# One step of a polynomial moved to GpSimd, K's placement to SyncE, and a new start, in a grouped-query attention kernel

**Chip, cores, metric.** One core of a Trainium2 chip (trn2). The metric is the device time of the whole program in microseconds (us): the median of several executions, each compared with executions of the kernel before on the same chip. A profiled execution also has a *span* in its trace.

## The reference

```python
q: (8, 8, 1024, 64)   k, v: (8, 2, 1024, 64)   float32; 4 query heads share one K and V
scores = (1/sqrt(64)) * q @ k^T
attn   = exp(scores - max) / sum(exp(scores - max))
output = attn @ v
```

There are 64 heads, each done as two *jobs* of 512 queries. A job has eight score tiles of 128 keys x 512 queries, so 1024 tiles ("cells") in all. Scores are small, so the kernel skips the maximum.

## The kernel before

TensorE makes each score cell into PSUM. Cells of kind A go to ScalarE, two per ACTIVATE. Cells of kind D go to VectorE: an eviction that scales the score into the bits of a bfloat16 power of two, then a correction of the mantissa for a whole group of cells:

```python
GROUP = 8
POOL_STEP = -1                       # no step of the chain on GpSimd
def exp_curve(g, m, step):           # all on VectorE
    if step == 0:   nc.vector.tensor_scalar(out=z, in0=pd, scalar1=0x7F, op0=ALU.bitwise_and)  # mask
    elif step == 1: nc.vector.tensor_scalar(out=y, in0=z, scalar1=CURVE_A / 128.0,
                                            scalar2=CURVE_B, op0=ALU.mult, op1=ALU.add)        # linear factor
    elif step == 2: nc.vector.tensor_tensor(out=y, in0=z, in1=y, op=ALU.mult)                  # product
    else:           nc.vector.tensor_tensor(out=pd, in0=pd, in1=y, op=ALU.add)                 # sum
```

A planner inside the kernel (`make_plan`) decides at build time which cells are A and which D, and in what order each engine works. It books a duration for every operation. Each engine then executes its list strictly in order.

Q and K are cast to bfloat16 through scratch memory by GpSimd's DMAs, transposed on load by SyncE's DMAs, and K is then copied to its two places:

```python
def place_k(b, g, side, parity):
    nc.gpsimd.dma_start(out=ksets[b % 2][...], in_=kT[(b, g)][...])      # 4 for each K, 60 in all
...
    for n in range(HALF // PIECE):
        at(th - 8.0 - 10.0 * spare + n, transpose_q, b, h, n)            # SyncE; th: planned first use
```

The first head does not wait for that path: TensorE transposes it, after 26 warm-up matmuls on a tile of zeros, and VectorE copies K to all its places.

The softmax here doesn't subtract the row's maximum and nothing guards it: scores larger than these inputs give would overflow.

Of the kernel before, what the change touches and what calls it, by code (L numbers as in the profile page):

```python
# [11 lines left out]

CURVE_A, CURVE_B = 0.32988085, -0.33401025

GROUP = 8
POOL_STEP = -1


def make_plan(nj, nkc):
# [5 lines left out]


    QK, PV, P1, NORM = 0.216, 0.1225, 0.603, 0.555
    EXP, AND, LINE, PRODUCT = (0.065, 0.4265), (0.20, 0.133), (0.20, 0.133), (0.16, 0.27)
    CHAIN = (AND, LINE, PRODUCT, PRODUCT)
    FROM_PE, FROM_ACT, FROM_DVE, FROM_POOL = 0.26, 0.17, 0.10, 0.15  # L30
    LIVE_A, LIVE_D, PENDING, PER_JOB, LEAD, RAMP, AHEAD, FIRST_PV = 28, 5, 16, 2, 6, 3, 0.08, 2.0
    INF = 1e9
    FIRST_LOAD, EACH_LOAD = 3.5, 4.0
    ops = []
    pe = act = dve = 0.0
    a_free, bank, obank_free = [0.0, 0.0], [0.0, 0.0], [0.0, 0.0]
# [18 lines left out]
    while normed < nj:  # L55
# [32 lines left out]
        for q, p, kind in ((normq, 0, "norm"), (p1q, 1, "p1"), (chainq, 2, "chain")):  # L88
            if q:
                at = q[0][0]  # L90
                if kind != "chain" or q[0][3] != POOL_STEP:
                    at = max(dve, at)
                best = min(best or (INF,), (at, p, kind, 0))
        if cur and job_d >= nj and not p1q:
# [2 lines left out]
        if kind == "qk":  # L97
            t = best[4]
            pe = t + QK
            j = job_d if arg else job_a  # L100
            cell = j * nkc + todo[j].pop(0)
            if not arg:
                if open_a is None:
                    slot = first_free(a_free)
                    a_id += 1
                    live["A"] += 1
                    open_a = {"slot": slot, "t": a_free[slot], "cells": []}
                    a_free[slot] = INF
                o = open_a
                ops.append((t, "qk", cell, "A", a_id, o["slot"], len(o["cells"])))  # L110
                o["cells"].append(cell)
                home[cell] = ("A", a_id)
                if len(o["cells"]) == 2 or not any(todo[job_a:]):
                    act = max(act, pe + FROM_PE)
                    ops.append((act, "exp", a_id, tuple(o["cells"])))
                    act += EXP[0] + EXP[1] * len(o["cells"])
                    a_free[o["slot"]] = act + FROM_ACT
                    uses[("A", a_id)] = len(o["cells"])
                    for x in o["cells"]:
                        ready[x] = act + FROM_ACT  # L120
                    open_a = None
            else:
                taken[j] += 1
                k = first_free(bank)
                bank[k] = INF
                pending += 1
                ops.append((t, "qk", cell, "D", k, 0, 0))
                p1q.append((pe + FROM_PE, cell, k))
        elif kind == "open":
            o = first_free(obank_free)  # L130
            obank[arg] = o
            obank_free[o] = INF
            open_jobs.append(arg)
            rem[arg] = list(range(nkc))
            next_job += 1
        elif kind == "pv":
            s, c = arg
            cell = s * nkc + c
            opens = len(rem[s]) == nkc
            rem[s].remove(c)  # L140
            done = not rem[s]
            ops.append((t, "pv", s, cell, opens, done, obank[s]))
            pe = t + PV
            h = home[cell]
            uses[h] -= 1
            if not uses[h]:
                live[h[0]] -= 1
            if done:
                open_jobs.remove(s)
                normq.append((pe + FROM_PE, s))  # L150
        elif kind == "norm":
            s = normq.pop(0)[1]
            ops.append((t, "norm", s))
            dve = t + NORM
            obank_free[obank[s]] = dve + FROM_DVE
            normed += 1
        elif kind == "p1":
            _, cell, k = p1q.pop(0)
            if not cur:
                d_id += 1  # L160
                live["D"] += 1
            ops.append((t, "p1", cell, k, d_id, len(cur)))
            dve = t + P1
            bank[k] = dve + FROM_DVE
            cur.append(cell)
            home[cell] = ("D", d_id)
            if len(cur) == GROUP:
                chainq.append((dve, d_id, cur, 0))
                cur = []
        elif kind == "flush":  # L170
            chainq.append((dve, d_id, cur, 0))
            cur = []
        else:
            _, g, cells, step = chainq.pop(0)
            ops.append((t, "chain", g, len(cells), step))
            end = t + CHAIN[step][0] + CHAIN[step][1] * len(cells)
            dve = end if step != POOL_STEP else dve
            if step + 1 < len(CHAIN):
                at = end + FROM_POOL if step == POOL_STEP else end
                at += FROM_DVE if step + 1 == POOL_STEP else 0.0  # L180
                chainq.insert(0, (at, g, cells, step + 1))
            else:
                pending -= len(cells)
                uses[("D", g)] = len(cells)
                for x in cells:
                    ready[x] = dve + FROM_DVE
# [4 lines left out]
def kernel(  # L191
# [7 lines left out]
    nc = tc.nc  # L199
# [17 lines left out]
    NQS = QBS // 128  # L217
    E1 = D + 1
    PIECE = 256
    WARM = 26  # L220
    SECOND = 0.45
    CAST_GAP = 3.0
    scale = 1.0 / math.sqrt(D)
    bits_scale = 128.0 * scale * math.log2(math.e)
    bits_bias = 128.0 * 127.0
# [4 lines left out]

    jobs = [(b, h, side) for b in range(B) for h in range(H) for side in range(2)]
    plan = make_plan(len(jobs), NKC)

    const_pool = ctx.enter_context(tc.tile_pool(name="constp", bufs=1))
    scr_pool = ctx.enter_context(
# [19 lines left out]
    apools, dbanks, obanks = psum_pools("aps", 2), psum_pools("dps", 2), psum_pools("ops", 2)  # L255

    blank = const_pool.tile([128, 128], BF16)
    nc.vector.memset(blank, 0.0)  # L258
    ident = const_pool.tile([128, 128], BF16)
    make_identity(nc, ident)  # L260
    vsets, ksets = [], []
# [11 lines left out]

    def at(t, f, *args):
        events.append((t, len(events), f, args))

    qT = {}
    kT = {}
# [24 lines left out]
        transpose(("k", b, g), kT[(b, g)], n)  # L303

    def place_k(b, g, side, parity):
        nc.gpsimd.dma_start(  # L306
            out=ksets[b % 2][
                side * D : (side + 1) * D, g, side, parity * HALF : (parity + 1) * HALF
            ],
# [18 lines left out]
    def first_loads():  # L328
# [46 lines left out]
        for n, half in enumerate(halves):  # L375
            nc.scalar.copy(out=hk[:, half, 0:2, :], in_=fk[:, half])  # L376
            nc.vector.tensor_copy(
                out=hq[:, half], in_=fq[:, half].rearrange("p c two d -> p c (two d)")
            )
            turn_k(0, half)  # L380
            keep_warm(2)
            for c in range(NHC)[half]:
                nc.tensor.transpose(tq[:, c * 128 : (c + 1) * 128], hq[:, c, :], ident)  # L383
            keep_warm(2)
            if n == 0:
                cast(("q", 0, 2), q[0, 2])
        for half in halves:
            cols = slice(half.start * 128, half.stop * 128)
            nc.scalar.copy(out=qT[(0, 0)][:, cols], in_=tq[:, cols])  # L389
            put_k(0, 0, half)  # L390
        def second():
            every = slice(0, NHC)
            turn_k(1, every)
            for side, parity in ((0, 1), (1, 0), (1, 1)):
                put_k(side, parity, every)

        nc.vector.tensor_copy(out=hk[:, :, 2, :], in_=fk[:, :, 0, :])
        at(SECOND, second)

    p_of = {}  # L400
    psum = {}
# [43 lines left out]

    def exp_curve(g, m, step):
        pd = groups[g][:, 0:m]
        if step == 0:
            z = tmp_pool.tile([128, GROUP, QBS], U16, name="z")[:, 0:m]
            temps[g] = [z]  # L450
            nc.vector.tensor_scalar(  # L451
                out=z, in0=pd, scalar1=0x7F, scalar2=None, op0=ALU.bitwise_and
            )
        elif step == 1:
            y = tmp_pool.tile([128, GROUP, QBS], FP16, name="y")[:, 0:m]
            temps[g].append(y)
            nc.vector.tensor_scalar(  # L457
                out=y,
                in0=temps[g][0],
                scalar1=CURVE_A / 128.0,  # L460
# [3 lines left out]
            )  # L464
        elif step == 2:
            z, y = temps[g]
            nc.vector.tensor_tensor(out=y, in0=z, in1=y, op=ALU.mult)  # L467
        else:
            y = temps.pop(g)[1]
            groups.pop(g)  # L470
            nc.vector.tensor_tensor(out=pd, in0=pd, in1=y, op=ALU.add)  # L471

    def output_mms(s, cell, opens, closes, bk):
        b, h, side = jobs[s]
# [13 lines left out]
    def normalise(s):  # L488
# [1 line left out]
        o = ops_of.pop(s)  # L490
        rec = recip_pool.tile([128, NQS], FP32, name="rec")
        nc.vector.reciprocal(out=rec, in_=o[:, :, D])  # L492
        if side == 0:
            stage[(b, h)] = ostage_pool.tile([128, NQS, 2, D], FP32, name="ost")
        nc.vector.tensor_tensor(  # L495
            out=stage[(b, h)][:, :, side, :],
# [9 lines left out]
            in_=stage[(b, h)][:, :, sides],  # L506
        )

    first_use = {}
    run = {"qk": score, "exp": exps, "p1": exp_bits, "chain": exp_curve,  # L510
           "pv": output_mms, "norm": normalise}
    for op in plan:
        if op[1] == "qk":
            first_use.setdefault(op[2] // (2 * NKC), op[0])
        elif op[1] == "norm":
            b, h, side = jobs[op[2]]
            if op[2] >= len(jobs) - 2:
                at(op[0] + 0.01, put_out, b, h, slice(side, side + 1))
            elif side:
                at(op[0] + 1.5, put_out, b, h, slice(0, 2))  # L520
        at(op[0], run[op[1]], *op[2:])

# [4 lines left out]
    for b in range(B):  # L527
        for h in range(H):
# [8 lines left out]
            if h % HPG == 0:  # L537
# [6 lines left out]
                    for parity in range(2):  # L544
                        at(th - 6.0 - 9.0 * spare, place_k, b, g, side, parity)
                for two in range(2):
                    at(th - 4.0 - 8.0 * spare + two, place_v, b, g, two)
    casts.sort(key=lambda e: e[0])
    latest = 1e9
    for n in reversed(range(len(casts))):  # L550
# [3 lines left out]
    for t, key, src in casts:  # L554
        t = max(t, soonest)
        soonest = t + 2.0
        at(t, cast, key, src)
    with tc.manual_schedule():
        first_loads()
        for _, _, f, args in sorted(events, key=lambda e: e[:2]):  # L560
# [31 lines left out]
```

## Time and profile before

Time before: 393.41 us (three runs, 393.38 to 393.47). The one run that left the first trace took 395.51 us, with a span of 393.7 us.

| | busy, of a span of 393.7 us | what it does |
|---|---|---|
| ScalarE (ACT) | 380.7 us, 97% | 411 exponentials, 822 cells |
| TensorE (PE) | 371.0 us, 94% | scores, outputs |
| VectorE (DVE) | 366.2 us, 93% | 202 cells, 128 normalisations |
| GpSimd (POOL) | 107.1 us, 27% | DMA issues |

A group line of the page reads: line, engine, operation, output<-input, shapes, count | busy time, mean ns of one | idle time of the engine just before, and what ended it. The prediction below shows these lines and reads them.

### The profile page before, as it was taken

The page shows a single profiled execution, that of the slowest core. Times are in us where ns is not written, and L with a number is a line of the kernel's source. Part 1 is how long each engine was busy: PE and PEld are TensorE (multiplying, and loading weights), DVE is VectorE, ACT ScalarE, POOL GpSimd, SP SyncE. Part 2 cuts the span into 40 slices and gives each one's busy share as a digit, 9 for nine tenths or more (in the row PEclk, how much of TensorE's full clock was granted, in tenths as well). Part 3 has the DMA queues.
Part 4 walks back from the last instruction along what each step waited for, and adds up shares of the span by engine and source line. Part 5 has one row for each costly group of instructions (what it writes and reads, how often), then busy time and mean ns, then how long its engine had stood idle before and what let it go on. Part 6 is the DMA issues. An engine that isn't in the chain of part 4 may idle for free.

```text
span 393.7 us, 12506 instructions
## 1 busy us (share of the span) xinstructions
PE 371.0 (94%) x5166; PEld 234.3 (60%) x5166; DVE 366.2 (93%) x573; ACT 380.7 (97%) x416; POOL 107.1 (27%) x184
## 2 busy tenths in 40 slices
PE   7989999999999999999999999999999999999995
PEld 5435556566666566566566566566556556556664
DVE  3799999999999999999999999999999999999992
ACT  4799999999999999999999999999999999999994
POOL 4285241413205032141413305032331416000000
PEclk9999999999999999999999999999999999999999
DMA  7499995756959559394665868468595658520113
GB/s 120 87 169 203 140 142 101 148 80 126 156 100 148 109 111 148 91 156 86 123 107 116 143 117 132 105 115 134 103 133 105 130 87 148 101 72 28 55 55 82
DMA packets 101992, 45.39 MB, mean 115 GB/s; under 512 B 66256, under 2 KB 99536, under 8 KB 100688
## 3 DMA queue, kind: packets, MB, share of 16 engines
q0 software_dynamic: 21600, 17.05, 34.9%
q1 hardware_dynamic: 79792, 27.29, 30.5%
q8 instruction: 40, 0.66, 0.7%
q10 hardware_dynamic: 544, 0.26, 0.2%
q14 instruction: 16, 0.13, 0.1%
HBM read 25.17 MB, written 27.00 MB: 133 GB/s over the span
## 4 chain that ended last, share of the span: by engine, by line
ACT 81%; PE 11%; issue 6%; DMA 1%; DVE 0%
ACT pa L427 80%; PE aps L416 5%; PE ops L479 4%; PE dps L416 2%; DMA fk<-in_k_dram 1%; DVE kset L350 0%; PE dps L341 0%; ACT qT L389 0%; PE ops L368 0%; PE dps L383 0%; DVE ost L495 0%; ACT hk L376 0%; DVE rec L492 0%
## 5 line engine op out<-in xcount | busy, mean ns | idle before, releaser
L427 ACT ACTIVATE pa<-aps 128x1024 bf16<-128x1024 f32 x411 | 378.0, 1064 | 3.9 <-PE aps L416 3.8
L416 PE MATMUL aps<-qT,kset 128*128 128x512 bf16 x822 | 245.8, 380 | 15.8 <-ACT pa L427 13.8
L479 PEld LDWEIGHTS <-pa 128*128 128x128 bf16 x3288 | 137.6, 98 | 61.1 <-issue 1.1
L479 PE MATMUL ops<-vset,pa 128*128 128x65 bf16 x3288 | 149.1, 194 | 0.0
L436 DVE TENSOR_SCALAR pd<-dps 128x512 uint16<-128x512 f32 x202 | 130.9, 682 | 3.7 <-PE dps L416 3.1
L416 PEld LDWEIGHTS <-kset 128*128 128x128 bf16 x1024 | 82.6, 98 | 73.4 <-issue 37.4
L286 POOL DMA_DIRECT2D scr_q<-in_q_dram x63 | 34.4, 545 | 201.5 <-PE aps L416 152.2
L416 PE MATMUL dps<-qT,kset 128*128 128x512 bf16 x202 | 71.4, 383 | 1.2 <-DVE kset L350 0.9
L495 DVE TENSOR_TENSOR ost<-ops,rec 128x256 f32<-128x256 f32 x128 | 54.3, 424 | 4.4
L471 DVE TENSOR_TENSOR pd<-pd,y 128x4096 uint16<-128x4096 uint16 (+1 forms) x26 | 57.8, 2224 | 0.3
L467 DVE TENSOR_TENSOR y<-z,y 128x4096 f16<-128x4096 uint16 (+1 forms) x26 | 57.7, 2220 | 0.1
L479 PEld LDWEIGHTS <-pd 128*128 128x128 bf16 x808 | 36.5, 97 | 18.3 <-DVE pd L471 0.6
L479 PE MATMUL ops<-vset,pd 128*128 128x65 bf16 x808 | 41.3, 193 | 0.0
L306 POOL DMA_DIRECT2D kset<-kT x60 | 34.5, 584 | 1.4 <-issue 0.4
L457 DVE TENSOR_SCALAR y<-z 128x4096 f16<-128x4096 uint16 (+1 forms) x26 | 31.5, 1210 | 0.0
L451 DVE TENSOR_SCALAR z<-pd 128x4096 uint16<-128x4096 uint16 (+1 forms) x26 | 31.3, 1202 | 0.0
L492 DVE RECIPROCAL rec<-ops 128x4 f32<-128x4 f32 x128 | 22.6, 176 | 9.0 <-PE ops L479 7.7
L319 POOL DMA_DIRECT2D vset<-in_v_dram x32 | 26.4, 831 | 2.1 <-issue 1.9
L286 POOL DMA_DIRECT2D scr_k<-in_k_dram x15 | 8.1, 540 | 28.1 <-PE aps L416 22.2
L368 PE MATMUL ops<-blank 128*128 128x128 bf16 x34 | 4.6, 312 | 1.0 <-DVE blank L258 1.0
L368 PEld LDWEIGHTS <-blank 128*128 128x128 bf16 x34 | 3.7, 148 | 1.0 <-DVE blank L258 1.0
L350 DVE COPY kset<-dps 64x512 bf16<-64x512 bf16 (+1 forms) x5 | 1.7, 365 | 2.8 <-PE dps L341 2.7
(19 smaller groups left out, 12.6 us busy)
## 6 DMA issues: line engine op xcount, KB each, us to landing
out_dram<-ost SPq DMA_DIRECT2D x63, 256.0 KB, 3.2
scr_q<-in_q_dram POOLq DMA_DIRECT2D x63, 128.0 KB, 3.2
kset<-kT POOLq DMA_DIRECT2D x60, 64.0 KB, 3.4
vset<-in_v_dram POOLq DMA_DIRECT2D x32, 64.0 KB, 4.9
qT<-scr_q SPq DMA_TRANSPOSE x126, 4.0
scr_k<-in_k_dram POOLq DMA_DIRECT2D x15, 128.0 KB, 3.2
kset<-kset POOLq DMA_DIRECT2D x6, 128.0 KB, 4.9
kT<-scr_k SPq DMA_TRANSPOSE x30, 4.0
```

The source lines that it names most:

```text
L286: dma = nc.gpsimd.dma_start(out=scr.rearrange("(p f) -> p f", f=1024), in_=src.rearrange("(p s) d -> p (s d)", s=1024 // D),)
L306: nc.gpsimd.dma_start(out=ksets[b % 2][side * D : (side + 1) * D, g, side, parity * HALF : (parity + 1) * HALF], in_=kT[(b, g)][parity * D ...
L319: nc.gpsimd.dma_start(out=vsets[b % 2][:, g, two * NHC : (two + 1) * NHC, 0:D], in_=v[b, g].rearrange("(c p two) d -> two p c d", p=128, t ...
L416: last_score[0] = nc.tensor.matmul(dst, lhsT=ksets[b % 2][:, h // HPG, side, c * 128 : (c + 1) * 128], rhs=qT[(b, h)], start=True, stop=Tr ...
L427: nc.scalar.activation(out=pt[:, 0:m], in_=psum.pop(("A", n))[:, 0:m], func=AF.Exp, scale=scale)
L436: nc.vector.tensor_scalar(out=groups[g][:, slot], in0=psum.pop(cell), scalar1=bits_scale, scalar2=bits_bias, op0=ALU.mult, op1=ALU.add,)
L451: nc.vector.tensor_scalar(out=z, in0=pd, scalar1=0x7F, scalar2=None, op0=ALU.bitwise_and)
L457: nc.vector.tensor_scalar(out=y, in0=temps[g][0], scalar1=CURVE_A / 128.0, scalar2=CURVE_B, op0=ALU.mult, op1=ALU.add,)
L467: nc.vector.tensor_tensor(out=y, in0=z, in1=y, op=ALU.mult)
L471: nc.vector.tensor_tensor(out=pd, in0=pd, in1=y, op=ALU.add)
L479: nc.tensor.matmul(ops_of[s][:, qs, :], lhsT=p_of[cell][:, qs * 128 : (qs + 1) * 128], rhs=vsets[b % 2][:, h // HPG, c, :], start=opens an ...
L495: nc.vector.tensor_tensor(out=stage[(b, h)][:, :, side, :], in0=o[:, :, 0:D], in1=rec.unsqueeze(2).to_broadcast([128, NQS, D]), op=ALU.mult,)
```

## The change

The intent: VectorE and ScalarE are both full, GpSimd is not. Give GpSimd one step of VectorE's chain, so that VectorE can take cells from ScalarE. GpSimd's DMAs must then neither delay that step nor be delayed by it, so K's placements leave GpSimd, and its other DMAs are planned around the step. Separately, the start is rearranged to keep TensorE busy until the first scores.

```diff
-GROUP = 8
-POOL_STEP = -1
+GROUP = 10
+POOL_STEPS = (1,)
...
-    EXP, AND, LINE, PRODUCT = (0.065, 0.4265), (0.20, 0.133), (0.20, 0.133), (0.16, 0.27)
+    EXP = (0.065, 0.4265)
+    CHAIN = ((0.20, 0.133), (0.25, 0.43), (0.16, 0.27), (0.16, 0.27))
...   (planner: 20 pending cells for 16, D cells up to 8 jobs ahead for 6 and reached more
       slowly, each head's load booked some 1 us later at the start, 4.2 us apart for 4.0;
       a head is stored when the later of its two jobs is done)
+    def at_pool(t, f, *args):
+        for first, last in chains:               # the planned GpSimd steps
+            if first - POOL_DMA < t < last:
+                t = last + 0.01
+        at(t, f, *args)
...
     def place_k(b, g, side, parity):
-        nc.gpsimd.dma_start(
+        nc.sync.dma_start(
...
     def exp_curve(g, m, step):
+        eng = nc.gpsimd if step in POOL_STEPS else nc.vector
...   (casts of Q and K, and loads of V: at -> at_pool)
-    nc.vector.memset(blank, 0.0)
+    nc.vector.memset(blank, 1.0)
-    WARM = 26
+    WARM = 30
...   (head: Q's second half copied by VectorE, not ScalarE; four more warm-ups
       before the first score; K for side 1 by one GpSimd DMA, not VectorE copies)
+        last_score[0] = keep_warm(4)
+        put_k(0, 1, slice(0, NHC))
+        nc.gpsimd.dma_start(out=ksets[0][hi, 0, 1, :], in_=ksets[0][lo, 0, 0, :])
```

More of the change, by code (lines that the diff above doesn't have):

```diff
@@ L13 @@
 CURVE_A, CURVE_B = 0.32988085, -0.33401025
-GROUP = 8
-POOL_STEP = -1
+GROUP = 10
+POOL_STEPS = (1,)
 def make_plan(nj, nkc):
     QK, PV, P1, NORM = 0.216, 0.1225, 0.603, 0.555
-    EXP, AND, LINE, PRODUCT = (0.065, 0.4265), (0.20, 0.133), (0.20, 0.133), (0.16, 0.27)
-    CHAIN = (AND, LINE, PRODUCT, PRODUCT)
+    EXP = (0.065, 0.4265)
+    CHAIN = ((0.20, 0.133), (0.25, 0.43), (0.16, 0.27), (0.16, 0.27))
     FROM_PE, FROM_ACT, FROM_DVE, FROM_POOL = 0.26, 0.17, 0.10, 0.15
-    LIVE_A, LIVE_D, PENDING, PER_JOB, LEAD, RAMP, AHEAD, FIRST_PV = 28, 5, 16, 2, 6, 3, 0.08, 2.0
+    LIVE_A, LIVE_D, PENDING, PER_JOB, LEAD, RAMP, AHEAD, FIRST_PV = 28, 5, 20, 2, 8, 6, 0.08, 2.0
     INF = 1e9
-    FIRST_LOAD, EACH_LOAD = 3.5, 4.0
+    FIRST_LOAD, EACH_LOAD = 4.5, 4.2
     ops = []
@@ L90, in make_plan @@
                 at = q[0][0]
-                if kind != "chain" or q[0][3] != POOL_STEP:
+                if kind != "chain" or q[0][3] not in POOL_STEPS:
                     at = max(dve, at)
@@ L167, in make_plan @@
             if len(cur) == GROUP:
-                chainq.append((dve, d_id, cur, 0))
+                chainq.append((dve + FROM_DVE * (0 in POOL_STEPS), d_id, cur, 0))
                 cur = []
         elif kind == "flush":
-            chainq.append((dve, d_id, cur, 0))
+            chainq.append((dve + FROM_DVE * (0 in POOL_STEPS), d_id, cur, 0))
             cur = []
@@ L176, in make_plan @@
             end = t + CHAIN[step][0] + CHAIN[step][1] * len(cells)
-            dve = end if step != POOL_STEP else dve
+            dve = end if step not in POOL_STEPS else dve
             if step + 1 < len(CHAIN):
-                at = end + FROM_POOL if step == POOL_STEP else end
-                at += FROM_DVE if step + 1 == POOL_STEP else 0.0
+                at = end
+                if (step in POOL_STEPS) != (step + 1 in POOL_STEPS):
+                    at += FROM_POOL if step in POOL_STEPS else FROM_DVE
                 chainq.insert(0, (at, g, cells, step + 1))
@@ L219 @@
     PIECE = 256
-    WARM = 26
-    SECOND = 0.45
+    WARM = 30
     CAST_GAP = 3.0
+    POOL_DMA = 1.0
     scale = 1.0 / math.sqrt(D)
@@ L232 @@
     plan = make_plan(len(jobs), NKC)
+    starts = {}
+    for op in plan:
+        if op[1] == "chain" and op[4] in POOL_STEPS:
+            starts.setdefault(op[2], []).append(op[0])
+    chains = sorted((min(t), max(t)) for t in starts.values())
     const_pool = ctx.enter_context(tc.tile_pool(name="constp", bufs=1))
@@ L379, in first_loads @@
             )
+            nc.vector.tensor_copy(out=hk[:, half, 2, :], in_=fk[:, half, 0, :])
             turn_k(0, half)
@@ L383, in first_loads @@
                 nc.tensor.transpose(tq[:, c * 128 : (c + 1) * 128], hq[:, c, :], ident)
-            keep_warm(2)
             if n == 0:
+                keep_warm(2)
                 cast(("q", 0, 2), q[0, 2])
-        for half in halves:
+        for copy, half in zip((nc.scalar.copy, nc.vector.tensor_copy), halves):
             cols = slice(half.start * 128, half.stop * 128)
-            nc.scalar.copy(out=qT[(0, 0)][:, cols], in_=tq[:, cols])
             put_k(0, 0, half)
-        def second():
-            every = slice(0, NHC)
-            turn_k(1, every)
-            for side, parity in ((0, 1), (1, 0), (1, 1)):
-                put_k(side, parity, every)
-        nc.vector.tensor_copy(out=hk[:, :, 2, :], in_=fk[:, :, 0, :])
-        at(SECOND, second)
+            copy(out=qT[(0, 0)][:, cols], in_=tq[:, cols])
+        turn_k(1, slice(0, NHC))
+        last_score[0] = keep_warm(4)
+        put_k(0, 1, slice(0, NHC))
+        nc.gpsimd.dma_start(out=ksets[0][hi, 0, 1, :], in_=ksets[0][lo, 0, 0, :])
     p_of = {}
@@ L450, in exp_curve @@
             temps[g] = [z]
-            nc.vector.tensor_scalar(
+            eng.tensor_scalar(
                 out=z, in0=pd, scalar1=0x7F, scalar2=None, op0=ALU.bitwise_and
@@ L456, in exp_curve @@
             temps[g].append(y)
-            nc.vector.tensor_scalar(
+            eng.tensor_scalar(
                 out=y,
@@ L466, in exp_curve @@
             z, y = temps[g]
-            nc.vector.tensor_tensor(out=y, in0=z, in1=y, op=ALU.mult)
+            eng.tensor_tensor(out=y, in0=z, in1=y, op=ALU.mult)
         else:
@@ L470, in exp_curve @@
             groups.pop(g)
-            nc.vector.tensor_tensor(out=pd, in0=pd, in1=y, op=ALU.add)
+            eng.tensor_tensor(out=pd, in0=pd, in1=y, op=ALU.add)
     def output_mms(s, cell, opens, closes, bk):
@@ L492, in normalise @@
         nc.vector.reciprocal(out=rec, in_=o[:, :, D])
-        if side == 0:
+        if (b, h) not in stage:
             stage[(b, h)] = ostage_pool.tile([128, NQS, 2, D], FP32, name="ost")
@@ L507, in put_out @@
         )
-    first_use = {}
+    first_use, ended = {}, {}
     run = {"qk": score, "exp": exps, "p1": exp_bits, "chain": exp_curve,
@@ L518 @@
                 at(op[0] + 0.01, put_out, b, h, slice(side, side + 1))
-            elif side:
+            elif ended.setdefault(op[2] // 2, op[2]) != op[2]:
                 at(op[0] + 1.5, put_out, b, h, slice(0, 2))
@@ L546 @@
                 for two in range(2):
-                    at(th - 4.0 - 8.0 * spare + two, place_v, b, g, two)
+                    at_pool(th - 4.0 - 8.0 * spare + two, place_v, b, g, two)
     casts.sort(key=lambda e: e[0])
@@ L556 @@
         soonest = t + 2.0
-        at(t, cast, key, src)
+        at_pool(t, cast, key, src)
     with tc.manual_schedule():
```

## The prediction

> **What bounds the kernel now.** I read the page first: busy shares, then the chain that ended last, then the costliest groups.
>
> ```profile
> PE 371.0 (94%) x5166; PEld 234.3 (60%) x5166; DVE 366.2 (93%) x573; ACT 380.7 (97%) x416; POOL 107.1 (27%) x184
> ...
> ACT 81%; PE 11%; issue 6%; DMA 1%; DVE 0%
> ...
> L427 ACT ACTIVATE pa<-aps 128x1024 bf16<-128x1024 f32 x411 | 378.0, 1064 | 3.9 <-PE aps L416 3.8
> L436 DVE TENSOR_SCALAR pd<-dps 128x512 uint16<-128x512 f32 x202 | 130.9, 682 | 3.7 <-PE dps L416 3.1
> L471 DVE TENSOR_TENSOR pd<-pd,y 128x4096 uint16<-128x4096 uint16 (+1 forms) x26 | 57.8, 2224 | 0.3
> L467 DVE TENSOR_TENSOR y<-z,y 128x4096 f16<-128x4096 uint16 (+1 forms) x26 | 57.7, 2220 | 0.1
> L457 DVE TENSOR_SCALAR y<-z 128x4096 f16<-128x4096 uint16 (+1 forms) x26 | 31.5, 1210 | 0.0
> L451 DVE TENSOR_SCALAR z<-pd 128x4096 uint16<-128x4096 uint16 (+1 forms) x26 | 31.3, 1202 | 0.0
> ```
>
> The 1024 score tiles of 128x512 ("cells") are exponentiated in two ways. ScalarE takes 822 cells, two per ACTIVATE. VectorE takes 202 by the bit trick: one eviction each, then a chain of four wide steps (mask, linear factor, product, sum) over eight cells. ScalarE owns 81% of the last chain and has only 3.9 us of idle time before its exponentials. VectorE is nearly as full. So ScalarE is the bound, and relieving VectorE helps only by the cells that it then takes from ScalarE.
>
> Second, ScalarE in order of time, to cut the span in pieces, and a window of the middle (columns: length, PE, PEld, DVE, ACT, POOL, granted clock, DMA).
>
> ```profile
> 7.53 1.02 ACT L427 ACTIVATE pa<-aps 128x1024 bf16<-128x1024 f32 x1 [1.10 <-PE aps L416]
> 8.81 1.02 ACT L427 ACTIVATE pa<-aps 128x1024 bf16<-128x1024 f32 x1 [0.26 <-PE aps L416]
> 11.58 1.02 ACT L427 ACTIVATE pa<-aps 128x1024 bf16<-128x1024 f32 x1 [1.75 <-PE aps L416]
> ...
> 40.00:120.00 80.00, 77.89 (x1123) 49.85 (x1121) 77.94 (x122) 80.00 (x88) 20.77 (x37) 1.00 0.73 122
> ...
> 369.82 18.51 ACT L427 ACTIVATE pa<-aps 128x1024 bf16<-128x1024 f32 x20
> ```
>
> The first exponential starts at 7.53, then three gaps (0.26, 1.75 and 0.70 us) follow, and from 13.30 ScalarE never rests: 80.00 of 80 us in the window. It ends at 369.82 + 18.51 = 388.33. So 408 exponentials take 388.33 - 13.30 = 375.0 us, **0.919 us each** (1.064 us is the length of one, they overlap). The tail after it is 393.7 - 388.33 = 5.4 us: last outputs, normalisation, store.
>
> Third, TensorE in that head.
>
> ```profile
> 6.48 1.44 PE L416 MATMUL aps<-qT,kset 128*128 128x512 bf16 x3 [0.52 <-ACT qT L389]
> ...
> 9.66 1.03 PE L416 MATMUL dps<-qT,kset 128*128 128x512 bf16 x2 [0.89 <-DVE kset L350]
> 10.48 1.06 PE L416 MATMUL aps<-qT,kset 128*128 128x512 bf16 x2
> ...
> 14.82 0.59 PE L416 MATMUL aps<-qT,kset 128*128 128x512 bf16 x2
> ```
>
> Two scores take 1.06 us at 10.48 and 0.59 us at 14.82: a score issues every 0.43 us until about 13.5 and every 0.216 us after. That half speed, plus the wait for K's second side at 9.66, makes the gaps on ScalarE. The granted clock column says 1.00 there all the same, so I go by durations.
>
> **What the Trainium skill says.** "TensorE: Matmul & The Clock Gate", Part 1: the array runs at half clock until it was busy through a window of about 3.4 us. The trace agrees: warm-up matmuls from 1.00 to 3.95 (2.95 us), a gap, work to 5.96, a gap, half speed; busy from 9.66 on, full speed from about 13.5, after 3.8 us. "GPSIMD Engine Reference", section 3.1: a body of up to two operations runs at 1.03 cycles per element, and the specifications give 1.2 GHz; no wide GpSimd arithmetic is in the trace of before. "SBUF — State Buffer", "Two separate sides": GpSimd and VectorE lock each other out of a shared port pair only when VectorE runs a two-port mode or has two SBUF inputs. The trace cannot confirm it.
>
> **The change part by part.** I compared the two instruction orders for counts.
>
> *Chain.* The linear factor leaves VectorE: 31.5 us less. Cells on VectorE go from 202 to 212: ten evictions at about 0.60 us (in the timeline two of them start 1.20 us before the next operation), 6 us more. Mask and products in tens: the forms of 1024 and 4096 elements take 420 and 1233 ns (mask) and about 690 and 2283 ns (products), so 5120 elements should take 1.5 and 2.8 us; 21 full chains and one of two cells cost about what 26 cost now (+1 us). VectorE: 366.2 - 31.5 + 6 + 1 = **342 us**. It gets 24 us of slack and the order hands it only ten cells.
>
> *ScalarE.* 812 cells, 406 exponentials instead of 411: 5 x 0.919 = **4.6 us less on the path**.
>
> *GpSimd.* A step of 5120 elements: 5120 x 1.03 / 1.2 GHz = 4.4 us, say 4.6 us with its dispatch (an estimate from the skill's page). The kernel's plan books 0.25 + 10 x 0.43 = 4.55 us. In the order of the changed kernel 19 of the 21 chains of ten (not the first and the last) have 5 to 7 evictions and 2 or 3 normalisations (0.55 us each: two span 1.09 us) between mask and product: 4.1 to 5.9 us of VectorE work, mean 5.0. With semaphores (my guess 0.2 us) the step needs 4.8, so ten of these chains leave VectorE idle by 0.1 to 0.7 us; with 24 us of slack that should not reach ScalarE. Evictions and normalisations read PSUM and have at most one SBUF input, so I expect no lock conflict. Total on GpSimd: 22 steps, about 96 us beside its DMA issues of 72 us after the move of 34.5 us of K placement.
>
> *K over SyncE.* 60 issues of about 0.55 us are 33 us on a queue whose listed waits sum to 192 us. Placements precede their use by 6 to 15 us against 3.4 us to landing. Hidden; nothing gained or lost.
>
> *Head.* 30 warm-up matmuls from 1.0 (about 0.105 us each, to 4.2), then transposes and ten more warm-ups without a gap to the first score at about 6.4: 5.4 us busy, against 2.95 before. The array should be at full speed by the first scores. First exponential at about 7.2. The side-1 copy of K is now one GpSimd DMA, issued about 6.5 when the copy it reads is done; 3 to 3.5 us to landing, about 9.8. The ninth score needs it; ScalarE, with three exponentials in hand, runs dry at about 10.0 and resumes at about 10.5. So some 0.8 us of gaps replace 2.7, and the start is 0.3 earlier: **2.2 us less**.
>
> *Sum.* 7.2 + 406 x 0.919 (373.2) + 0.8 + tail 5.3 = 386.5 span; I add 0.6 for exposed stalls and subtract 0.3, since the median is 0.3 below the traced span: **386.8 us**, 1.7% below 393.41.
>
> **The rivals.** (a) *GpSimd becomes a wait.* If its step takes 5.5 us rather than 4.6, most chains hold VectorE about half a microsecond; VectorE executes in order, the two PSUM banks of its cells fill, TensorE stops and ScalarE has only two buffers: up to 8 us back, 391 to 394. For: TensorE has little room (77 of 80 us). Against: the plan's number and the page agree. (b) *The head stays at half speed*, if transposes do not count as busy or the window falls badly: ScalarE starves as before until 13.5, about 2 us back, 388.8. (c) *K's DMA lands later* (wide K copies take 4.9 us in this trace): another microsecond. (d) *Everything fits*: no gaps at all, 385.5. (e) The early Q transposes, issued gaplessly by SyncE until 31 us, now stand behind K placements: a microsecond if a head comes late.
>
> **Range and chances.** (d) to (b) with a margin for (c) and (e): 384.8 to 389.6. Faster by over 2% means below 385.5, which needs all parts at their best: 0.20. Within 2%: 0.77. Slower needs (a) several times over: 0.03.
>
> **What would show it.** 406 exponentials at 0.919 us with almost no idle time in the middle; VectorE busy near 342 us; the GpSimd step at 4.4 to 4.7 us, VectorE waiting for it under 6 us in all; scores 0.216 us apart from the first; ScalarE's only gap about 10 us into the run, on K's DMA. I am wrong if ScalarE waits on TensorE in the middle while VectorE waits on GpSimd, or if a wide VectorE step or eviction gets longer beside GpSimd.

## The result

The changed kernel took **390.12 us** (four runs, 389.85 to 391.14) against 393.39 (four runs, 393.16 to 393.47): a ratio of 0.9923, with a 95% interval of 0.9904 to 0.9941. A ratio is the mean time of one kernel's fast runs over that of the other's in the same rounds, so it is not quite the ratio of the medians. The gain of 3.3 us is half the predicted 6.6, and the time lies above the range.

The page of the changed kernel: busy line, chain of waits by line, and the groups concerned.

```profile
PE 362.7 (93%) x5080; PEld 234.1 (60%) x5172; DVE 350.6 (90%) x545; ACT 376.5 (97%) x410; POOL 166.6 (43%) x147
...
ACT pa L437 66%; PE aps L426 7%; PE ops L490 6%; DMA qT<-scr_q 3%; PE dps L426 3%; DVE pd L446 2%; SPq L311 1%; DMA scr_q<-in_q_dram 1%; DMA kset<-kT 1%; DVE ost L506 1%; DVE pd L482 1%; DVE y L478 1%; SPq L319 1%; DVE z L462 0%; DVE rec L503 0%
...
L437 ACT ACTIVATE pa<-aps 128x1024 bf16<-128x1024 f32 x406 | 374.0, 1060 | 5.1 <-PE aps L426 4.3
...
L446 DVE TENSOR_SCALAR pd<-dps 128x512 uint16<-128x512 f32 x212 | 138.1, 684 | 14.3 <-PE dps L426 13.4
L468 POOL TENSOR_SCALAR y<-z 128x5120 f16<-128x5120 uint16 (+1 forms) x22 | 94.6, 4300 | 89.7 <-DVE z L462 54.9
...
L478 DVE TENSOR_TENSOR y<-z,y 128x5120 f16<-128x5120 uint16 (+1 forms) x22 | 59.8, 2719 | 0.1
```

The chain part did what it should: 406 exponentials, a GpSimd step of 4.45 us at ten cells (4.30 is the mean with the short last one), and 0.1 us of idle time before the product that waits for it. Evictions stay at 684 ns beside GpSimd, against 682. But DMAs now take a larger part of the chain of waits (5% for 1%): Q's transposes, K's placement, SyncE's queue. ScalarE in order of time shows where they bite. (Columns: start, length, engine, line, operation, tiles, shapes, count, and in brackets the idle time before it.)

```profile
6.98 2.85 ACT L437 ACTIVATE pa<-aps 128x1024 bf16<-128x1024 f32 x3 [1.02 <-PE aps L426]
10.46 6.52 ACT L437 ACTIVATE pa<-aps 128x1024 bf16<-128x1024 f32 x7 [0.62 <-PE aps L426]
17.26 51.76 ACT L437 ACTIVATE pa<-aps 128x1024 bf16<-128x1024 f32 x56 [0.27 <-PE aps L426]
69.91 13.93 ACT L437 ACTIVATE pa<-aps 128x1024 bf16<-128x1024 f32 x15 [0.89 <-PE aps L426]
84.87 22.16 ACT L437 ACTIVATE pa<-aps 128x1024 bf16<-128x1024 f32 x24 [1.03 <-PE aps L426]
```

The head is as predicted: a first exponential at about 7, one gap at about 10. The gaps at 69.9 and 84.9 us are new; the kernel before had none past 17 us. What TensorE waited for in this trace (total us, times, longest):

```profile
PE dps L426 <- DMA qT<-scr_q: 1.5, 2, 1.1
...
PE dps L426 <- DMA kset<-kT: 0.5, 1, 0.5
```

The stop before 84.9 us is Q's. For the stop before 69.9 the profile names VectorE, which had then been done for 0.2 us; the first K placement for that head landed at 68.79 us, 7.1 us after its issue, and the score began at 68.88. So that stop is K's.

In the prediction's own parts, this trace has 6.98 us to the first exponential (7.2 predicted), 378.2 from there to the end of the last (374.0, plus 0.6 allowed for stalls) and a tail of 4.25 (5.3). The four stops between 17 and 155 us are 2.7 us of the excess in the middle.

Three questions follow. Why did a head that came out as predicted gain so little? Why does Q come late? And is there anything else?

### The profile page after: what moved, and what is told of

It is laid out like the page before. It is cut to its first block, busy times and chain, and to the rows that moved or that the text cites. A ratio compares the mean times of both kernels' runs of the same rounds, so it can differ in the third digit from the quotient of the medians.

```text
span 389.4 us, 12414 instructions
## 1 busy us (share of the span) xinstructions
PE 362.7 (93%) x5080; PEld 234.1 (60%) x5172; DVE 350.6 (90%) x545; ACT 376.5 (97%) x410; POOL 166.6 (43%) x147
## 3 DMA queue, kind: packets, MB, share of 16 engines
q0 software_dynamic: 19728, 13.25, 30.4%
## 4 chain that ended last, share of the span: by engine, by line
ACT 66%; PE 16%; issue 6%; DMA 5%; DVE 5%; SPq 2%; POOL 0%; POOLq 0%; ACTq 0%
ACT pa L437 66%; PE aps L426 7%; PE ops L490 6%; DMA qT<-scr_q 3%; PE dps L426 3%; DVE pd L446 2%; SPq L311 1%; DMA scr_q<-in_q_dram 1%; DMA kset<-kT 1%; DVE ost L506 1%; DVE pd L482 1%; DVE y L478 1%; SPq L319 1%; DVE z L462 0%; DVE rec L503 0%
## 5 line engine op out<-in xcount | busy, mean ns | idle before, releaser
L437 ACT ACTIVATE pa<-aps 128x1024 bf16<-128x1024 f32 x406 | 374.0, 1060 | 5.1 <-PE aps L426 4.3
L426 PE MATMUL aps<-qT,kset 128*128 128x512 bf16 x721 | 221.4, 378 | 13.0 <-ACT pa L437 11.3
L446 DVE TENSOR_SCALAR pd<-dps 128x512 uint16<-128x512 f32 x212 | 138.1, 684 | 14.3 <-PE dps L426 13.4
L468 POOL TENSOR_SCALAR y<-z 128x5120 f16<-128x5120 uint16 (+1 forms) x22 | 94.6, 4300 | 89.7 <-DVE z L462 54.9
L478 DVE TENSOR_TENSOR y<-z,y 128x5120 f16<-128x5120 uint16 (+1 forms) x22 | 59.8, 2719 | 0.1
L482 DVE TENSOR_TENSOR pd<-pd,y 128x5120 uint16<-128x5120 uint16 (+1 forms) x22 | 59.8, 2720 | 0.1
L490 PEld LDWEIGHTS <-pd 128*128 128x128 bf16 x848 | 40.5, 97 | 24.7 <-DVE pd L482 2.3
L490 PE MATMUL ops<-vset,pd 128*128 128x65 bf16 x848 | 46.3, 194 | 1.0
L503 DVE RECIPROCAL rec<-ops 128x4 f32<-128x4 f32 x128 | 22.7, 177 | 13.2 <-PE ops L490 12.3
L462 DVE TENSOR_SCALAR z<-pd 128x5120 uint16<-128x5120 uint16 (+1 forms) x22 | 31.6, 1436 | 0.1
L339 POOL DMA_DIRECT2D kset<-kset x6 | 4.1, 694 | 0.0
```

Of the source, the lines that this page charges most:

```text
L426: last_score[0] = nc.tensor.matmul(dst, lhsT=ksets[b % 2][:, h // HPG, side, c * 128 : (c + 1) * 128], rhs=qT[(b, h)], start=True, stop=Tr ...
L437: nc.scalar.activation(out=pt[:, 0:m], in_=psum.pop(("A", n))[:, 0:m], func=AF.Exp, scale=scale)
L446: nc.vector.tensor_scalar(out=groups[g][:, slot], in0=psum.pop(cell), scalar1=bits_scale, scalar2=bits_bias, op0=ALU.mult, op1=ALU.add,)
L462: eng.tensor_scalar(out=z, in0=pd, scalar1=0x7F, scalar2=None, op0=ALU.bitwise_and)
L468: eng.tensor_scalar(out=y, in0=temps[g][0], scalar1=CURVE_A / 128.0, scalar2=CURVE_B, op0=ALU.mult, op1=ALU.add,)
L478: eng.tensor_tensor(out=y, in0=z, in1=y, op=ALU.mult)
```

## The experiments

Twelve kernels, each in six runs, with eleven runs of the kernel before beside each set of four. The medians of the kernel before were 393.24, 393.59 and 392.91 us in the three sets. The sets ran on three different chips; the fast starts of the kernel before averaged 393.0, 393.2 and 392.9 us in them, so a comparison across sets is good to about 0.3 us. All runs but one are marked fast (y3's slowest is marked slow, for being over 1.5% above the fastest of its kernel).

### Set 1: the head, and who places K

**x1: the kernel before, once more.** No edit.

> The kernel before, unchanged. Its first traced run had a span of 393.7 us at 395.51 us, while its timed runs took 393.2 to 393.5. Theory A (the traced run had an unlucky head, TensorE at half speed until 13.5 us; the timed runs mostly do not): this trace is likely to have a span near 391.6 us and TensorE at full speed before 8 us, so three to four exponentials run without gaps from 7.5 us. Theory B (tracing or the first execution adds about 2 us anywhere): the head again has the gaps 0.26, 1.75 and 0.70 us. Times near 393.4 either way.

Measured 393.24 us (392.69 to 395.36). Its traced run took 393.25, with a span of 391.4 us, 2.3 us below the first trace. ScalarE in order of time:

```profile
6.70 1.94 ACT L427 ACTIVATE pa<-aps 128x1024 bf16<-128x1024 f32 x2 [0.68 <-PE aps L416]
9.49 1.02 ACT L427 ACTIVATE pa<-aps 128x1024 bf16<-128x1024 f32 x1 [0.85 <-PE aps L416]
10.68 5.65 ACT L427 ACTIVATE pa<-aps 128x1024 bf16<-128x1024 f32 x6 [0.17 <-PE aps L416]
```

The fourth exponential starts at 10.68 us; in the first trace, the same kernel's started at 13.30. The trace's clock records have TensorE at full speed from 4.2 us here, and from 13.7 there. Over all 44 runs of the kernel before, ten took 395.3 to 395.8 us, one 394.1, and the rest 392.5 to 393.7. So a run of this kernel seems to draw between two starts, and the first trace showed the rarer one. Theory A holds, as far as two traces and the two groups of times show it.

**x2: the kernel before with the new head alone.**

```diff
 kernel before, with:
+    blank of ones, WARM = 30, the changed kernel's order of transposes, warm-ups and copies,
+    nc.gpsimd.dma_start(out=ksets[0][hi, 0, 1, :], in_=ksets[0][lo, 0, 0, :])
```

> The kernel before with the new head alone (30 warm-ups of ones, no gap to the first score, side 1 of K by a DMA). Theory A: at most 0.8 us faster than before, about 392.6 to 393.4. Theory B, and my prediction's 2.2 us: about 391.2.

Measured 394.16 us (393.58 to 394.92): no gain, rather 0.9 us more than the median before, above both theories' windows. No run has the slow start's 395.3 or more. Six runs alone would not settle that, but in all nine traces with the new head TensorE is at full speed by 7.1 us. So the new head seems to remove the bad draw, and costs something in the good one. That cost is not in the head: at the twentieth exponential this trace is still 0.36 us ahead of x1's. But from there on the interval between exponentials is longer by 0.2 to 0.3 us, 1.5 us in all, at 45.0, 103.9, 162.9, 221.8, 280.7 and 339.7 us. The spacing is 58.9 us, which is 64 exponentials. The changed kernel's trace has the same stutter; x1 and the first trace have none.

**x3: the changed kernel with the old head.** The reverse of x2.

```diff
 changed kernel, with:
-    the new head
+    blank of zeros, WARM = 26, VectorE copies of K for side 1 at 0.45, as in the kernel before
```

> The changed kernel with the old head. Theory A: within 0.8 us of the changed kernel, 390.0 to 390.9. Theory B: 2 us slower than the changed kernel, about 392.

Measured 391.4 us, but from 388.43 to 393.95: a miss of theory A's window in both directions. The traced run (390.61) had no stutter, and one long gap in which Q came late:

```profile
85.50 1.02 ACT L441 ACTIVATE pa<-aps 128x1024 bf16<-128x1024 f32 x1 [2.53 <-PE aps L430]
87.10 297.49 ACT L441 ACTIVATE pa<-aps 128x1024 bf16<-128x1024 f32 x324 [0.58 <-PE aps L430]
```

During that stop, in which TensorE was idle for 1.74 us, its clock fell to one half for 3.4 us, the clock records say, and the gap of 0.58 follows. So a late load can cost more than itself. The other five runs left no trace; what set them apart (slow starts, late loads) is not known run by run. Two of them (388.43 and 389.29) lie below every run of the changed kernel, as they may without the stutter.

**x4: the changed kernel with K placed by GpSimd again,** clear of its steps.

```diff
-        nc.sync.dma_start(            # place_k
+        nc.gpsimd.dma_start(
-  at(th - 6.0 - 9.0 * spare, place_k, ...)
+  at_pool(th - 6.0 - 9.0 * spare, place_k, ...)
```

> The changed kernel with K put in place by GpSimd again, kept clear of its arithmetic. If the Q and K transfers that come late (gaps of 1.03 and 0.48 us before exponentials in the changed kernel's trace) come from K placements in SyncE's queue: those gaps vanish and the time falls by 1 to 1.5 us to about 388.8. If GpSimd is short of time with both, its step starts late, VectorE waits, and it is slower than 390.1.

Measured 392.0 us (389.68 to 392.49): half a miss. The gaps at 69 to 85 us are gone, but there is one of 1.43 us at 31.7 us. The chain of waits there runs from the first GpSimd step (to 24.4 us) through four DMA issues behind it to K's placement at 26 us and its landing at 30.3. The first K needed through this path is too urgent to stand behind that step. The traced run was one of the two fast ones. The other four took 391.6 to 392.5 us with a mean granted clock of 0.994 to 0.996, for 0.998 and 0.999; a stretch of 3.4 us at half speed, as in x3, would lower the mean by 0.004. That a late K stopped TensorE longer in them is likely, not shown.

**How late Q comes.** I matched SyncE's transfers and TensorE's weight loads in the traces with the instruction orders. For each of the 63 heads after the first this gives the time from the landing of its Q to its first score; and, summed over SyncE's issues, how long that queue was issuing.

| traced run | Q lands before use, median | heads under 2 us | Q's cast landed, to its transpose | SyncE issuing |
|---|---|---|---|---|
| before, x1 | 13.2 us | 3 | 3.7 us | 260 us |
| changed kernel | 4.8 us | 15 | 10.4 us | 310 us |
| x4, K by GpSimd | 12.8 us | 0 | 3.0 us | 259 us |

The loads are cast in time; they then stand in SyncE's queue. Here is that queue in the kernel before (x1), and then in the changed kernel, in the same stretch. Each line is a run of issues: start, length, what, how many.

```profile
119.85 0.53 SPq L504 DMA_DIRECT2D out_dram<-ost  x1
120.87 2.58 SPq L298 DMA_TRANSPOSE qT<-scr_q  x2
126.21 0.37 SPq L504 DMA_DIRECT2D out_dram<-ost  x1
126.69 2.92 SPq L298 DMA_TRANSPOSE qT<-scr_q  x2
```

```profile
119.99 0.53 SPq L515 DMA_DIRECT2D out_dram<-ost  x1
120.57 5.86 SPq L311 DMA_TRANSPOSE qT<-scr_q  x3
126.48 2.51 SPq L319 DMA_DIRECT2D kset<-kT  x4
129.09 1.27 SPq L515 DMA_DIRECT2D out_dram<-ost  x1
```

Before, the queue pauses (2.8 us between 123.4 and 126.2). In the changed kernel each line starts 0.1 us or less after the last one ended: in this stretch it does not pause, and so does not catch up with what it lost before. It recovers only near the end, where heads past the 50th land some 9 to 15 us early again.

### Set 2: one cause at a time

**y1: K over SyncE alone,** in the kernel before.

```diff
-        nc.gpsimd.dma_start(            # place_k, kernel before
+        nc.sync.dma_start(
```

> The kernel before with one part of the change: K put in place over SyncE. Theory C (SyncE's in-order queue, already issuing for some 265 of 391 us, falls behind by the 60 placements of about 0.7 us each): SyncE issues for over 300 us, the time between the landing of a Q transfer and its first use falls from a median of 13 us to about 5, and a few scores wait for Q; 0.5 to 2 us slower than before, in some runs more. My prediction (hidden): no gap on ScalarE after 17 us and the time of before, 393.2.

Measured 397.12 us (396.77 to 398.08), **3.5 us slower** than before: worse than theory C's 0.5 to 2. SyncE issued for 311 us and Q's median fell to 8.0 us. Most of the loss is one stop:

```profile
31.90 1.02 ACT L427 ACTIVATE pa<-aps 128x1024 bf16<-128x1024 f32 x1 [3.35 <-PE aps L416]
```

Here the four placements of the second K were issued from 22.9 us and landed at 29.0 to 30.2, 5.4 to 6.1 us later; in x1 GpSimd issued them from 22.7 us and they landed at 25.7 to 27.3. GpSimd, relieved, had meanwhile issued its other copies and loads sooner, so they were in flight together. That this is why they took longer is argued, not shown: in the first trace GpSimd's own four took 5.1 to 5.5 us, without a stop, since the start ran later there. And K was issued in time. So y1 shows that moving K costs this kernel time in all six runs; that SyncE's full queue is the reason for the stop it does not show. The kernel before has no room for a slow landing here: in x1 the last piece of this K landed at 27.34 us, and its first score came at 27.45. TensorE's clock fell to one half here too, until 32.9 us.

**y2: K over SyncE for the first batch, by GpSimd after that,** in the changed kernel. That leaves SyncE one K, four of the 60 placements.

```diff
-        nc.sync.dma_start(
+        (nc.sync if b == 0 else nc.gpsimd).dma_start(
-  at(th - 6.0 - 9.0 * spare, place_k, ...)
+  (at_pool if b else at)(th - 6.0 - 9.0 * spare, place_k, ...)
```

> The changed kernel with K over SyncE for the first batch alone, and by GpSimd, clear of its arithmetic, after that. Theory C: Q lands 12 us or more before use as in before, the gaps of 0.5 to 1.2 us on ScalarE past 40 us are gone, and the time is 388.5 to 389.5 with little spread. If the gaps come from the wide steps on GpSimd instead, they stay, and the time is 390 or more.

Measured **388.42 us** (387.89 to 388.91), 1.7 us below the changed kernel (1.9, if each is set against the kernel before in its own rounds), and with a spread of 1.0 us. Q lands 12.8 us before use. No gap is left past the head except the stutter, whose larger steps the timeline shows:

```profile
10.28 94.28 ACT L437 ACTIVATE pa<-aps 128x1024 bf16<-128x1024 f32 x102 [0.59 <-PE aps L426]
104.74 176.86 ACT L437 ACTIVATE pa<-aps 128x1024 bf16<-128x1024 f32 x192 [0.17 <-ACT pa L437]
281.78 100.35 ACT L437 ACTIVATE pa<-aps 128x1024 bf16<-128x1024 f32 x109 [0.19 <-ACT pa L437]
```

192 is three times 64. The engine waits for "itself": nothing that the profile knows.

**y3: the changed kernel with one ScalarE instruction more.** The new head has one copy fewer on ScalarE than the old one. This puts one in front, in idle time.

```diff
+        one = first_pool.tile([128, 1], BF16, name="one")
+        nc.scalar.copy(out=one, in_=blank[:, 0:1])
```

> The changed kernel with one more tiny copy on ScalarE ahead of everything, while it waits for its first input. Theory D (the stutter of 0.27 us every 64th exponential, every 58.9 us, that shows in all kernels with the new head and none with the old one, comes from where ScalarE's instructions lie, since the new head has one instruction less there): the six stutters vanish, about 1.5 us faster than the changed kernel, 388.6. If the stutter comes from another part of the head (the DMA copy of K, say): they stay, 390.1.

The stutter is gone from the trace. The time does not tell: 389.89 us, from 387.5 to 394.09 (389.13 and up to 392.31 without the slow run). Late K and Q probably scatter the runs: its trace has gaps of up to 0.9 us, and 20 heads whose Q landed less than 2 us before use.

**y4: both mends.** y2 and y3 together, two lines changed and two added in the changed kernel.

> Both mends together. Theories C and D: no gap on ScalarE past 20 us, 406 exponentials at 0.918 us, 387.3 to 388.3, so 1.3 to 1.5% below the kernel before. If only one holds, about 389.

Measured **386.99 us** (386.61 to 387.78), a ratio of 0.9825 to the kernel before (0.9798 to 0.9853, so at 2% the verdict is "unclear"): the lowest median of the study, below every run of the kernel before and of the changed kernel. Against y2 the ranges do not touch, so the instruction is worth 1.4 us. Its ScalarE:

```profile
10.38 157.04 ACT L439 ACTIVATE pa<-aps 128x1024 bf16<-128x1024 f32 x171 [0.64 <-PE aps L428]
167.67 213.05 ACT L439 ACTIVATE pa<-aps 128x1024 bf16<-128x1024 f32 x232 [0.26 <-PE aps L428]
```

From 10.38 to 380.72 us there is one gap of 0.26 us. ScalarE is the bound again. Of the 6.5 us between x1's span and this one, 4.6 are the five saved exponentials and 1.1 a shorter tail.

### Set 3: the other parts, on the mended kernel (y4)

**z1: GpSimd's DMAs not kept clear.** `at_pool` does what `at` does.

> The mended kernel (K of the first batch over SyncE, later K by GpSimd, one tiny ScalarE copy more; 387.0 us) without keeping GpSimd's transfers clear of its arithmetic: they are issued when planned. If keeping clear matters, up to four K issues (2.1 us) stand ahead of a linear factor, VectorE waits for it by 1 us or more in several chains and scores wait for VectorE: 388 to 389. If the 1 us of slack in the chains takes it up: 387.0 within 0.4.

Measured 389.04 us (388.73 to 389.63): 2.1 us slower. VectorE now waits for the step, in four chains:

```profile
DVE y L479 <- POOL y L469: 2.8, 4, 1.8
```

Its traced run also had a late start (first exponential at 7.59 us for 6.88), so 0.7 of the 2.6 us between the two spans is not this.

**z2: the old head on the mended chain and transfers.**

> The same chain and transfers as the mended kernel, with the old head (26 warm-ups, side 1 of K by VectorE copies, no tiny copy). Theory A: in some three quarters of its runs TensorE is at full speed by the first scores and the time is within 0.5 us of the mended kernel's 387.0; in one quarter it starts at half speed and takes 2 to 2.5 us more, about 389.3. No stutter every 64th exponential, since this head has the old number of ScalarE instructions.

Measured 387.15 us: five runs at 387.03 to 387.53 and one at 389.98. So the old head, where its start is fast, equals the new one within the 0.3 us between sets, and the slow draw costs 2.5 to 3 us (that run left no trace). Its traced run has no stutter. This is theory A's picture with nothing else in the way.

**z3: chains of eight.** `GROUP = 8`.

> The mended kernel with chains of eight. The order then hands VectorE 211 cells instead of 212 and 27 chains instead of 22: about 5 x 4 fixed costs of 0.15 us more, 3 us more on VectorE, and fewer operations between mask and product to cover the GpSimd step of 3.6 us. If ScalarE stays the bound: 407 exponentials, 387.5 to 388. If VectorE's lateness reaches the scores: 389 or more.

Measured 390.33 us (389.53 to 391.0), 3.3 us slower. The step takes 3.60 us, and VectorE waits for it in 12 chains:

```profile
DVE y L480 <- POOL y L470: 7.6, 12, 1.4
```

But these waits hardly reach ScalarE, whose last stop ends at 86.7 us:

```profile
86.71 296.08 ACT L439 ACTIVATE pa<-aps 128x1024 bf16<-128x1024 f32 x323 [0.61 <-PE aps L428]
```

The 3.7 us between this span and y4's are one exponential more (0.9), a tail of 5.9 us for 4.3 (1.6), a later first exponential (0.7: 7.60 for 6.88) and only 0.4 of gaps. Nine of the twelve waits, 4.7 us together, come after 90 us, with no stop behind them.

**z4: a longer GpSimd step.** Two of ten tenths are written twice.

```diff
+            if m == GROUP:
+                eng.tensor_scalar(out=y[:, 0:2], in0=z[:, 0:2], ...)   # the same values again
```

> The mended kernel with two tenths of the linear factor written a second time by GpSimd, same values: its step grows from 4.45 to about 5.4 us. My rival (a) said that a step of 5.5 us would cost up to 8 us, since most chains have only 4.1 to 5.9 us of other work on VectorE in between. If so: 390 or more. If VectorE's slack takes it up, under 1 us: 387.0 to 388.

Measured 394.18 us (393.55 to 394.29), **7.2 us slower**. The extra instruction takes 1.04 us in each of 21 chains:

```profile
DVE y L489 <- POOL y L479: 8.3, 11, 1.4
```

There were 8.3 us of waiting on VectorE and 7.2 us more of time (in the traces 6.5 of them between the first and the last exponential), with VectorE busy for only 89% of the span. The gaps on ScalarE past the start are spread over the run (ten, 0.2 to 1.4 us each, 5.4 in all), each 4 to 8 us after one of the waits. Rival (a) of the prediction is real; the change as built stands just short of it. Why z3's waits cost so little beside these is open; one difference is that z3's planner books its step at about its length (3.7 us for 3.6) and z4's does not (4.55 us for 5.5).

## Why the prediction was wrong

Step by step, in its own order:

- **The bound.** Right. Five exponentials fewer were worth 4.6 us: the mended kernel shows them undisturbed.
- **VectorE.** Predicted 342 us busy, measured 350.6. The ten evictions cost 7.2 us, not 6. I had the products at 2.8 us, which was right, but did not multiply them out: mask and products take 151.2 us for 146.8, 4.4 more where I wrote "+1 us" (my own figures give 4.8). Most of the rest is less overlap: the lengths of VectorE's operations exceed its busy time by 26.1 us, for 30.4 before. This was off the path and cost nothing. The conclusion "24 us of slack, so waits do not reach ScalarE" is not safe: in z4, with 42 us of idle time on VectorE, 8.3 us of waits came with a loss of 7.2.
- **GpSimd.** Predicted 4.6 us a step, measured 4.45. Predicted up to 0.7 us of wait in ten chains; there was 0.1 us in all. In the trace a step begins 0.10 us after the mask in most chains, so mask to product needs 4.6 us for the 4.8 that I counted; and of the 19 chains one had 4.0 us of VectorE work in between, the others 4.7 to 6.0 (predicted 4.1 to 5.9). No lock conflict shows: an eviction took 685 ns on average beside a step (103 of them) and 683 without (109). Products and sums never ran beside a step.
- **K over SyncE: "hidden; nothing gained or lost".** This step failed, and it is the first cause of the miss that lies in the change. I took the 192 us of listed waits as room. They are not: with 255 us of issuing they make 447 in a span of 393.7, so they overlap it. SyncE was issuing for some 260 of 391 us before, a Q transpose holds the queue for 1.23 us at the median, and a placement held it for 0.74 us on average (44.1 us over 60). At 310 us, in order, it does not catch up for 250 us. Rival (e) named the collision but gave it a microsecond at the start only. y2 shows the size: 1.7 us of the median, and x3 a single stop of 2.5 us.
- **Head: "2.2 us less".** The mechanism was right in every number (full speed by the first scores, first exponential at 6.98 for 7.2, a gap of 0.62 at 10 us on K's DMA), for this trace: in the nine traces with the new head full speed begins anywhere from 3.98 to 7.04 us and the first exponential from 6.77 to 7.60, so a smaller draw is left. The gain was not right, since the first trace showed a start that ten of 44 runs have. I had its time, 395.51 us, in hand beside a median of 393.41, and still wrote "the median is 0.3 below the traced span". In truth the time is 1.8 us *above* the span (391.14 against 389.4), and the traced run was 2.1 us slower than the median. My sum of spans, 387.1 us with the stalls, plus 1.8 would have been 388.9.
- **Not foreseen.** The stutter of about 0.28 us every 64 exponentials, +1.4 us (y4 against y2; 1.7 in the traces). And a tail of 4.25 us instead of 5.3, to the good: in the new order no full-head store stands between the last two half stores.

In medians, from the mended kernel back to the changed one: 387.0, with the stutter (y2) 388.4, with the late loads 390.1. Rival (d), everything fits, gave 385.5 in the prediction; with the right offset, 2.1 more, it lies 0.6 us above y4.

What stays open: why the stutter comes with one instruction less. Shown is that every trace whose head has one ScalarE instruction fewer has it (the changed kernel, x2, x4, y2), and none of the others (both traces of before, x3, y1, z2 with the old head; y3, y4, z1, z3 and z4 with the added copy). The traces say which place it is: 64 exponentials with the semaphore instructions between them are 128 of ScalarE's instructions, and in the four kernels with the stutter its 64th, 192nd, 320th instruction and so on is an exponential, the one that is late; in the ten other traces a semaphore instruction stands there, and the stutter is absent. Why that place costs 0.28 us, the fetching of instructions perhaps, is a guess. Nor was every part of the change tested alone: the planner's new spacing of loads came with the new chain in every run.

## What to carry to other kernels

Before a trace is used as a baseline, compare its own time with the median: if it is one of the slower runs, part of what it shows is not there to be gained. A queue that executes in order is an engine like any other: add up how long it is *issuing*, not how long it waits, before more transfers are given to it, and look at the time between landing and first use, which shrinks long before anything stalls. A step handed to another engine is surely free only as long as the work between its producer and its consumer covers it; beyond that its waits can reach the bound, however much slack the engine has in total (z4), though they need not (z3).

## What the Trainium skill lacked or had wrong

- "DMA: Bandwidth & Descriptors", section "Issuing engines are not separate DMA queues", says that the time on the sequencer to start a DMA is usually small relative to the DMA. Here it was not small: 1.23 us to issue a Q transpose that landed 3.6 us after its issue, 0.59 us (median) for a K placement that landed after 3.3. The queue was issuing for 310 of 389 us, and giving 56 of its DMAs back to GpSimd gained 1.7 us (y2).
- "TensorE: Matmul & The Clock Gate", Part 1, has the free-running window, and says the ramp matters for under 1% of a span. The penalty here is within that, 2 to 3 us of 393, but it lacks what this makes of repeated timings: the same kernel ran at 392.5 to 393.7 us in 33 of 44 runs and at 395.3 to 395.8 in ten. With the new head, some 5.4 us of nearly unbroken work from 1 us on, TensorE was at full speed by 7.1 us in all nine traces. And two stops in the middle, in which TensorE was idle for 1.74 us (x3) and 2.52 us (y1), each came with 3.4 us at half speed; one of 1.56 us (x4) did not.
- "GPSIMD Engine Reference", section 3.1: 1.03 cycles per element for a body of up to two operations (an estimate of 0.86 ns at its 1.2 GHz) is confirmed within 3%: 4.45 us for 5120 elements and 1.04 us for 1024 are 0.83 ns per element and about 0.19 us fixed. The page gives no total for the fixed part.
- No page has the stutter: about 0.28 us every 64 ACTIVATEs, 1.4 us in all, gone with one more tiny ScalarE instruction (y4 against y2).
